# A decoder step on one core: first right-hand block in its own tile, x by quarters, norm sums by token, w_out low parts from DRAM, a feed forward that begins with one half of the tokens

## Chip, core and metric

The kernel runs on one core of a Trainium2 chip. The metric is the device time of one execution in microseconds; the number quoted is the median of three. A profile of one execution shows what the engines did: TensorE (PE, matmuls; its weight loads are PEld), VectorE (DVE), ScalarE (ACT), GpSimd (POOL), and SyncE (SP), which issues the DMAs.

## What is computed

One layer of a decoder for 1024 prompt tokens and 8 single sample tokens, 1032 columns in all. The first half of the program (input projection, attention, pooling) is not touched. The part that matters here:

```
m = sigmoid(gate_a) * a + sigmoid(gate_b) * bb      # a: attention output through w_attn_o
x = x + gt1 * (m @ w_out)
h2 = _rmsnorm(x, g_norm2) * (1 + sc2) + sh2
gg, up = jnp.split(h2 @ w_gu, 2, axis=-1)
x = x + gt2 * ((jax.nn.silu(gg) * up) @ w_down)
```

The model width is 1024 (8 blocks of 128), the feed-forward width 2816 (22 blocks). All arithmetic is to f32 accuracy.

## The kernel before

**Products.** A matrix product of f32 accuracy is made of three matmuls: each operand is split into a high part (ACT copies it to the narrower type, line 100) and a low part (the difference, line 109, on DVE or POOL); high x high, high x low and low x high are summed in PSUM. In the feed forward, each product of 2x2 blocks is in addition computed with seven block products in place of eight, from sums and differences of blocks.

**Order.** The program is written as one list; a scheduler gives each engine its own queue, by priorities and estimates. Each queue runs strictly in its order: an instruction whose wait is open holds up all that stand behind it. The same holds for SP, which issues all the DMAs named here.

**Tokens by halves and quarters.** The columns are two halves i = 0 and 1 of 516, each two quarters of 258 (`T2` = 516, `HC` = 258). Matmuls here have 258 columns.

**`back`, first part.** `heads` loads an attention output of head pair k and half i from DRAM (`ot` from `o_d`) and splits it to `os`. For half 1 the three finished pairs are multiplied by `wo` while attention still runs, and ACT stores the result in `six` (lines 1070 to 1078). After attention, all of half 0 is multiplied (`pj`, 24 matmuls for each of 8 output blocks j), DVE applies gate a, POOL adds the gate b term (line 1052), and the result is split into `mh` and `ml`. For half 1, `rest` does the fourth pair while w_out runs on half 0.

**`back`, w_out and norm.** For half 0 and then half 1: eight blocks of `wout` are loaded and split (the low part by DVE or POOL, `WOE`; in both passes), multiplied by `mh` and `ml` (48 matmuls a block), DVE adds gate and residual (`x1a`, `x1b`), the result goes to `x1_d` in DRAM, ACT squares it (line 1199), the square is split into `sqh` and `sql`, and `stat` sums it over the partitions by matmuls with a matrix of ones (line 1173; the last block in f32, line 1170). `norm` takes the root (ACT) and the reciprocal (DVE, line 1104, 128 x 516), multiplies the eight blocks by it, applies scale and shift, and makes the seven combinations `cmb` of the feed forward's right-hand side. `norm(0)` runs beside the w_out pass of half 1; `norm(1)` runs when that pass is done, beside the feed forward's first group.

**`feed_forward`, groups.** 22 groups f, each 7 products x 2 halves x 12 = 168 matmuls, in PSUM tiles `fb`, `fa`, `fd`. Evictions: ACT copies `p1`, `u2`, `u4`; DVE line 1288 adds `p1` into the first entry of `stg`; lines 1301 and 1308 add to `u4`, `u2`; POOL multiplies. PE starts the sixth product on `fb` when `u4` has been copied out. `p1`, `u2`, `u4` have two buffers each, one for each half. In an even f the first right-hand block is written to entry 0 of `stg`; in the odd f the rest; at the end of the odd f DVE forms the sums (lines 1312 to 1315), and one DMA a half (line 1316, 903 KB) writes all seven entries to `cmb_d` in DRAM. `stg` has one buffer a half:

```
st = [ev.tile([P, 7, HC], F32, name="stg", tag=f"stg{i}", bufs=1) for i in range(2)]
```

Group 0 is followed by eight small `gate_late` products (`ada`); groups 1 to 12 also load w_down blocks and store their sums (`ws_d`).

**`feed_forward`, down.** Seven products o, each 264 matmuls (`fc`). Each needs eleven blocks `cml`, one for each pair of groups, loaded from `cmb_d`, split to `bh` and `bl`. `xacc` (eight loads of 516 KB, lines 1335 to 1339) brings x back from DRAM for the final sum.

## Time and profile before

| | |
|---|---|
| median of three runs | 1819.63 us (1814.4 to 1821.92) |
| the profiled execution | 1823.61 us |
| its span in the trace | 1821.8 us |
| mean granted PE clock over the span | 0.971 of full |

The trace is read as follows. Times in it are microseconds from the start of the span. Attention ends near 900, the w_out passes run from about 928 to 1058, the feed forward's group 0 from 1061, groups 1 to 21 from 1107.7 to 1578.4, the down product from there to the end at 1821.8. In a window row the count behind an engine's busy time includes instructions that overlap an edge. PEclk is the share of the full 2.4 GHz that PE was granted.

### The profile page before, as it was taken

The page shows a single profiled execution, that of the slowest core. Times are in us where ns is not written, and L with a number is a line of the kernel's source. Part 1 is how long each engine was busy: PE and PEld are TensorE (multiplying, and loading weights), DVE is VectorE, ACT ScalarE, POOL GpSimd, SP SyncE. Part 2 cuts the span into 40 slices and gives each one's busy share as a digit, 9 for nine tenths or more (in the row PEclk, how much of TensorE's full clock was granted, in tenths as well). Part 3 has the DMA queues.
Part 4 walks back from the last instruction along what each step waited for, and adds up shares of the span by engine and source line. Part 5 has one row for each costly group of instructions (what it writes and reads, how often), then busy time and mean ns, then how long its engine had stood idle before and what let it go on. Part 6 is the DMA issues. An engine that isn't in the chain of part 4 may idle for free. (4 is left out here: it accounts for less than half of the span.)

```text
span 1821.8 us, 34407 instructions
## 1 busy us (share of the span) xinstructions
PE 1688.4 (93%) x12936; PEld 1586.4 (87%) x12936; DVE 1014.5 (56%) x1947; ACT 773.5 (42%) x1875; POOL 527.5 (29%) x501
## 2 busy tenths in 40 slices
PE   6799999999999999998899879899989999969999
PEld 5799899789697899997799769899989999869999
DVE  6656756557241456557677865555454444545553
ACT  5433555445341445557634653333333333433431
POOL 2424201011011323222153526766564333100000
PEclk9899999999999999999999989899999999989999
DMA  9113634535635434214465325555552333665662
GB/s 372 63 58 104 218 99 136 172 111 155 194 114 182 155 122 128 95 65 131 129 213 164 112 86 188 178 169 177 171 169 87 93 112 111 203 235 171 222 195 75
DMA packets 172697, 270.12 MB, mean 148 GB/s; under 512 B 19017, under 2 KB 123106, under 8 KB 171506
## 3 DMA queue, kind: packets, MB, share of 16 engines
q1 hardware_dynamic: 172530, 267.92, 46.7%
q8 instruction: 102, 1.67, 0.4%
q14 instruction: 65, 0.53, 0.1%
HBM read 202.82 MB, written 65.04 MB: 147 GB/s over the span
## 5 line engine op out<-in xcount | busy, mean ns | idle before, releaser
L1255 PE MATMUL fb<-cmb,wst 128*128 128x258 f32 x704 | 207.9, 295 | 35.8 <-ACT u L1300 26.3
L1256 PE MATMUL fb<-cmb,wst 128*128 128x258 f32 x704 | 205.6, 292 | 0.7 <-DVE cmb L109 0.7
L1257 PE MATMUL fb<-cmb,wst 128*128 128x258 f32 x704 | 204.6, 291 | 0.0
L1255 PE MATMUL fc<-bh,wdn 128*128 128x258 f32 x616 | 174.4, 285 | 17.1 <-ACT bh L100 17.1
L1255 PEld LDWEIGHTS fb<-cmb,wst 128*128 128x128 f32 x704 | 139.7, 198 | 40.6 <-ACT u L1300 29.2
L1256 PE MATMUL fc<-bl,wdn 128*128 128x258 f32 x616 | 174.6, 284 | 0.0
L1257 PE MATMUL fc<-bh,wdn 128*128 128x258 f32 x616 | 173.1, 283 | 0.0
L70 PE MATMUL pj<-hh,wt_hi 128*128 128x344 f32 x480 | 159.4, 332 | 0.5 <-ACT u L546 0.5
L71 PE MATMUL pj<-hl,wt_hi 128*128 128x344 f32 x480 | 157.0, 327 | 0.0
L72 PE MATMUL pj<-hh,wt_lo 128*128 128x344 f32 x480 | 156.9, 327 | 0.0
L70 PE MATMUL kn<-wuh,lh 128*128 128x256 f32 (+1 forms) x512 | 150.4, 294 | 2.4 <-ACT nr L906 1.5
L71 PE MATMUL kn<-wul,lh 128*128 128x256 f32 (+1 forms) x512 | 145.3, 284 | 0.0
L72 PE MATMUL kn<-wuh,ll 128*128 128x256 f32 (+1 forms) x512 | 144.9, 284 | 0.0
L905 ACT ACTIVATE dsq<-kn 128x256 f32<-128x256 f32 x256 | 95.0, 380 | 111.2 <-PE kn L72 103.5
L1256 PEld LDWEIGHTS fb<-cmb,wst 128*128 128x128 f32 x704 | 139.7, 198 | 1.4 <-DVE cmb L109 1.4
L1257 PEld LDWEIGHTS fb<-cmb,wst 128*128 128x128 f32 x704 | 139.1, 198 | 0.0
L109 DVE TENSOR_TENSOR wst<-scm,wst 128x512 fp32r<-128x512 f32 x88 | 81.0, 922 | 93.2 <-ACT wst L100 91.7
L1255 PEld LDWEIGHTS fc<-bh,wdn 128*128 128x128 f32 x616 | 116.8, 190 | 17.5 <-ACT bh L100 17.3
L1256 PEld LDWEIGHTS fc<-bl,wdn 128*128 128x128 f32 x616 | 117.4, 191 | 0.0
L1257 PEld LDWEIGHTS fc<-bh,wdn 128*128 128x128 f32 x616 | 116.3, 190 | 0.3 <-DVE wdn L109 0.3
L907 DVE TENSOR_REDUCE ssq<-dsq 128x8 f32<-128x512 f32 x128 | 86.7, 679 | 53.0 <-ACT dsq L905 52.6
L70 PEld LDWEIGHTS kn<-wuh,lh 128*128 128x128 f32 x512 | 96.6, 189 | 13.5 <-issue 5.2
(397 smaller groups left out, 5106.5 us busy)
## 6 DMA issues: line engine op xcount, KB each, us to landing
fraw<-wgu_t SPq DMA_DIRECT2D x44, 512.0 KB, 4.1
cmb_d<-stg SPq DMA_DIRECT2D x22, 903.0 KB, 5.9
cml<-cmb_d SPq DMA_DIRECT2D x77, 258.0 KB, 3.5
pg<-cpack SPq DMA_DIRECT2D x128, 144.0 KB, 2.6
ln<-cnat SPq DMA_DIRECT2D x128, 128.5 KB, 2.3
wraw<-wada_t SPq DMA_DIRECT2D x24, 512.0 KB, 4.5
wraw<-win_t SPq DMA_DIRECT2D x20, 512.0 KB, 4.0
nat_d<-nat SPq DMA_DIRECT2D x8, 1024.0 KB, 4.5
```

The lines of the kernel that those rows point to most:

```text
L70: nc.tensor.matmul(out, sh, mh, start=first, stop=False)
L71: nc.tensor.matmul(out, sh, ml, start=False, stop=False)
L72: nc.tensor.matmul(out, sl, mh, start=False, stop=last)
L109: e.tensor_tensor(dl, src, dh.bitcast(F32), op=ALU.subtract)
L905: nc.scalar.activation(sq[:, half].rearrange("p h d -> p (h d)"), kn[:, o:o + 256], AF.Square)
L907: nc.vector.tensor_reduce(ssq[:, j, t], sq.rearrange("p a h d -> p (a h) d"), axis=AX.X, op=ALU.add)
L1255: nc.tensor.matmul(acc, sh, mh, start=first and not more, stop=False, **kw)
L1256: nc.tensor.matmul(acc, sh, ml, start=False, stop=False, **kw)
L1257: nc.tensor.matmul(acc, sl, mh, start=False, stop=last, **kw)
```

## The change

The change has five parts.

1. *w_o and gates.* `os` of half 0 for the first three pairs goes to tiles of pool M instead of tiles that weights use later, and so it may be split during attention. `six` now receives gate a from DVE (`gated`) and gate b from POOL during attention, so `rest` is one DVE operation and one POOL addition. The `pm` PSUM tile is two banks in one buffer.
2. *w_out low parts.* In the pass of half 0 each low part is also written to `wlo_d` in DRAM; in the pass of half 1 it is loaded from there and copied by ACT. The `wout` tiles rotate over three pairs instead of two.
3. *Norm sums.* POOL adds the squares of blocks 0 to 6 into `tot`; `rms` then sums `tot` and the last square over partitions with twelve matmuls of one column, the token on the output's partition; root and reciprocal are 86 x 6; six matmuls with the identity spread the result over the partitions, and DVE multiplies from PSUM.
4. *Feed forward.* The body of a group is a function of the halves; group 0 runs with half 0 alone, then the `ada` products, then half 1. The first right-hand block has its own tile `b11`, written by ACT and stored by its own DMA in the even f; `stg` has six entries and is opened in the odd f. Line 1292 of the new kernel adds in place in `p1`.
5. *x by quarters.* `xacc` is four loads of 1 MB, the first of them into a tile `xq` that is free when the w_down sums are done; each is issued ahead of the product that needs it.

```diff
+        wlo_d = self.dram.tile([8, P, 8, P], F32, name="wlo_d")
...
-            pm = r.enter_context(tc.tile_pool(name="pm", bufs=2, space=PSUM))
+            pm = r.enter_context(tc.tile_pool(name="pm", bufs=1, space=PSUM))
...
-            six = [m(f"c1_{8 + j}", "six") for j in range(8)]
+            six = [m(f"c1_{8 + j}", "part") for j in range(8)]
...
+                ot = m(f"c1_{22 + i}" if k == 3 else ("c1_22", "c1_23", "c0_23")[k], "ot")
                 nc.sync.dma_start(two(ot), seg(self.o_d[k], i))
-                if i == 0 and k < 3:
-                    z = self.W.tile([P, 2, T2], F32R, name="os", tag=f"w{k}")
-                    os[i][k] = [z[:, 0], z[:, 1]]
-                else:
-                    os[i][k] = [m(f"c0_{24 + 2 * i + n}" if k == 3 else f"c1_{2 * k + n}", "os", F32R) for n in range(2)]
+                os[i][k] = [m(f"c0_{24 + 2 * i + n}" if k == 3 else f"c1_{(0 if i else 16) + 2 * k + n}", "os", F32R)
+                            for n in range(2)]
                 self.split(*os[i][k], ot, "a")
...
+            def gated(t, g, acc):
+                nc.vector.scalar_tensor_tensor(two(t), two(g), 1.0, acc, op0=ALU.add, op1=ALU.mult)
...
             def rest(j):
                 t = self.sp.tile([P, T2], F32, name="mt", tag=f"s{j % 4}")
+                g = gate(self.sga_d, 1, j, xo.tile([P, T2], F32, name="sa2", tag=f"x{j}"))
+                acc = pm.tile([P, 2, 512], F32, name="pm", tag="pm")[:, :, :HC]
                 for h in range(2):
                     cs = slice(h * HC, (h + 1) * HC)
-                    acc = pm.tile([P, 512], F32, name="pm", tag="pm")[:, :HC]
-                    _mm3(nc, acc, *last(j), os[1][3][0][:, cs], os[1][3][1][:, cs], True, True)
-                    nc.vector.tensor_tensor(t[:, cs], acc, six[j][:, cs], op=ALU.add)
-                nc.vector.scalar_tensor_tensor(t, sa[1][j], 1.0, t, op0=ALU.add, op1=ALU.mult)
-                mix(1, j, t)
+                    _mm3(nc, acc[:, h], *last(j), os[1][3][0][:, cs], os[1][3][1][:, cs], True, True)
+                gated(t, g, acc)
+                mix(1, j, t, six[j])
...
+                g, b = (gate(d, 1, j, m(f"c0_{8 * n + j}", "early")) for n, d in enumerate((self.sga_d, self.gB_d)))
+                acc = pm.tile([P, 2, 512], F32, name="pm", tag="pm")[:, :, :HC]
                 for h in range(2):
                     cs = slice(h * HC, (h + 1) * HC)
-                    acc = pm.tile([P, 512], F32, name="pm", tag="pm")[:, :HC]
                     for k in range(3):
-                        _mm3(nc, acc, w[0][:, k], w[1][:, k], os[1][k][0][:, cs], os[1][k][1][:, cs], k == 0, k == 2)
-                    nc.scalar.activation(six[j][:, cs], acc, AF.Copy)
+                        _mm3(nc, acc[:, h], w[0][:, k], w[1][:, k], os[1][k][0][:, cs], os[1][k][1][:, cs], k == 0,
+                             k == 2)
+                gated(six[j], g, acc)
+                nc.gpsimd.tensor_tensor(six[j], six[j], b, op=ALU.add)
...
+            def rms(sums):
+                z = ps.tile([P, 2, 512], F32, name="st2", tag="mm")
+                n = HC // 3
+                for c in range(6):
+                    for q, t in enumerate(sums):
+                        nc.tensor.matmul(z[:n, 0, 300 + c:301 + c], t[:, c * n:c * n + n], self.ones[:, 0:1],
+                                         start=(q == 0), stop=(q == len(sums) - 1))
+                rs = xw.tile([P, 6], F32, name="rs2", bufs=1)
+                nc.scalar.activation(rs[:n], z[:n, 0, 300:306], AF.Sqrt, scale=1.0 / DM, bias=self.eps[:n])
+                nc.vector.reciprocal(rs[:n], rs[:n])
+                for c in range(6):
+                    nc.tensor.matmul(z[:, c // 3, c % 3 * n:c % 3 * n + n], rs[:n, c:c + 1].to_broadcast([n, P]),
+                                     self.ident[:n, :n], start=True, stop=True)
+                return z[:, :, :HC]
+            def norm(i, x1, sums, cm, tiles):
+                rb = rms(sums)
                 yield
                 def act(j):
                     x = x1[j]
-                    nc.vector.tensor_tensor(x, x, rs, op=ALU.mult)
+                    nc.vector.tensor_tensor(two(x), two(x), rb, op=ALU.mult)
...
+                tot = xw.tile([P, T2], F32, name="tot")
...
-                    wh, wlo = (self.W.tile([P, 8, P], F32R, name="wout", tag=f"w{3 + 2 * (j % 2) + n}") for n in range(2))
-                    self.split(wh, wlo, raw, "a", WOE[j])
+                    wh, wlo = (self.W.tile([P, 8, P], F32R, name="wout", tag=f"w{1 + 2 * (j % 3) + n}") for n in range(2))
                     if i == 0:
-                        gates_in(1, j)
+                        self.split(wh, wlo, raw, "a", WOE[j])
+                        nc.sync.dma_start(wlo_d[j], wlo.bitcast(F32))
+                    else:
+                        self.hi("a", wh, raw)
+                        raw = fw.tile([P, 8, P], F32, name="fraw")
+                        nc.sync.dma_start(raw, wlo_d[j])
+                        self.hi("a", wlo, raw)
...
-                    sq = xw.tile([P, T2], F32, name="sq2", bufs=1)
+                    sq = xw.tile([P, T2], F32, name="sq2") if j else tot
                     nc.scalar.activation(sq, x, AF.Square)
-                    if j == 7:
-                        sqs.append(sq)
-                    else:
-                        sqs.append([xw.tile([P, T2], F32R, name=z, tag=z) for z in ("sqh", "sql")])
-                        self.split(*sqs[j], sq, "a")
-                    if j:
-                        stat(j - 1)
+                    if 0 < j < 7:
+                        nc.gpsimd.tensor_tensor(tot, tot, sq, op=ALU.add)
                     for _ in range(3):
                         next(todo, None)
-                stat(7)
                 for _ in todo:
                     pass
                 self.comb.append(self.combos(i))
-                todo = norm(i, x1, st, self.comb[i], temps)
+                todo = norm(i, x1, (tot, sq), self.comb[i], temps)
...
-                if f % 2 == 0:
-                    st = [ev.tile([P, 7, HC], F32, name="stg", tag=f"stg{i}", bufs=1) for i in range(2)]
-                    b12 = [ev.tile([P, HC], F32, name="b12", tag=f"b12{i}", bufs=1) for i in range(2)]
-                    n1, n2 = [z[:, 0] for z in st], b12
-                else:
-                    n1, n2 = [z[:, 1] for z in st], [z[:, 5] for z in st]
-                b, p1, u2, u4, d = ([None, None] for _ in range(5))
-                for i in range(2):
+                for i in halves:
+                    if f % 2:
+                        st[i] = ev.tile([P, 6, HC], F32, name="stg", tag=f"stg{i}", bufs=1)
+                        n1[i], n2[i] = st[i][:, 0], st[i][:, 4]
+                    else:
+                        n1[i] = e1[i] = ev.tile([P, HC], F32, name="b11", tag=f"b11{i}", bufs=1)
+                        n2[i] = e2[i] = ev.tile([P, HC], F32, name="b12", tag=f"b12{i}", bufs=1)
+                for i in halves:
                     b[i] = bank("fb")[:, :HC]
                     run(b[i], 0, i)
                     p1[i] = t("p1")
...
-                    nc.vector.tensor_tensor(n1[i], a, p1[i], op=ALU.add)
-                for i in range(2):
+                    nc.vector.tensor_tensor(p1[i], a, p1[i], op=ALU.add)
...
-                    nc.scalar.activation(n1[i], n1[i], AF.Silu)
-                for i in range(2):
+                    nc.scalar.activation(n1[i], p1[i], AF.Silu)
...
-                    if f % 2:
+                    if f % 2 == 0:
+                        nc.sync.dma_start(self.cmb_d[0, f // 2, :, i], n1[i])
+                    else:
                         z, tt = st[i], nc.vector.tensor_tensor
-                        tt(z[:, 4], b12[i], z[:, 0], op=ALU.subtract)
-                        tt(z[:, 3], z[:, 5], b12[i], op=ALU.subtract)
-                        tt(z[:, 2], z[:, 5], z[:, 4], op=ALU.subtract)
-                        tt(z[:, 6], z[:, 1], z[:, 2], op=ALU.subtract)
-                        nc.sync.dma_start(self.cmb_d[:, f // 2, :, i].rearrange("o p n -> p o n"), z)
+                        tt(z[:, 3], e2[i], e1[i], op=ALU.subtract)
+                        tt(z[:, 2], z[:, 4], e2[i], op=ALU.subtract)
+                        tt(z[:, 1], z[:, 4], z[:, 3], op=ALU.subtract)
+                        tt(z[:, 5], z[:, 0], z[:, 1], op=ALU.subtract)
+                        nc.sync.dma_start(self.cmb_d[1:7, f // 2, :, i].rearrange("o p n -> p o n"), z)
+            for f in range(NF):
+                if f:
+                    w = weights(f)
+                    group(f, w, (0, 1))
+                else:
+                    group(f, w, (0,))
                 if f == 0:
                     for k in range(40, 48):
                         self.gate_late(k, ev, bank)
+                    group(f, w, (1,))
...
+        def xload(dm, h):
+            z = (xp if xs else xq).tile([P, 4, T2], F32, name="xacc", tag=f"xa{dm}_{h}" if xs else "xq")
+            nc.sync.dma_start(z, self.x1_d[dm:dm + 4][:, :, h * T2:(h + 1) * T2].rearrange("a p n -> p a n"))
+            for j in range(4):
+                xs[dm + j, h] = z[:, j]
...
+            if (dm, h) not in xs:
+                xload(dm, h)
```

**Order on DVE, turn of a pair of groups.** Before: the rows from the end of an odd f (`stg_15562`) to the even f that follows (`stg_16072`); `wst` are weight splits of the next group.

```order
L1315 TENSOR_TENSOR stg_15562<-stg_15562 128x258
L1315 TENSOR_TENSOR stg_15563<-stg_15563 128x258
L109 TENSOR_TENSOR wst_16303<-fraw_16291,wst_16303 128x512
L109 TENSOR_TENSOR wst_16306<-fraw_16291,wst_16306 128x512
L1288 TENSOR_TENSOR stg_16072<-fa_16106,p1_16089 128x258
L109 TENSOR_TENSOR wst_16309<-scm_16296,wst_16309 128x512
L1288 TENSOR_TENSOR stg_16073<-fa_16120,p1_16104 128x258
L109 TENSOR_TENSOR wst_16312<-scm_16297,wst_16312 128x512
L1301 TENSOR_TENSOR u4_16202<-fd_16162,u4_16202 128x258
L1301 TENSOR_TENSOR u4_16217<-fd_16176,u4_16217 128x258
```

Now, at a turn between an odd and an even f:

```order
L1321 TENSOR_TENSOR stg_15777<-stg_15777 128x258
L1321 TENSOR_TENSOR stg_15778<-stg_15778 128x258
L109 TENSOR_TENSOR wst_16270<-fraw_16258,wst_16270 128x512
L1292 TENSOR_TENSOR p1_16054<-fa_16071,p1_16054 128x258
L1292 TENSOR_TENSOR p1_16069<-fa_16085,p1_16069 128x258
L109 TENSOR_TENSOR wst_16273<-fraw_16258,wst_16273 128x512
L109 TENSOR_TENSOR wst_16276<-scm_16263,wst_16276 128x512
L109 TENSOR_TENSOR wst_16279<-scm_16264,wst_16279 128x512
L1305 TENSOR_TENSOR u4_16167<-fd_16127,u4_16167 128x258
L1305 TENSOR_TENSOR u4_16182<-fd_16141,u4_16182 128x258
```

Before, the sum behind the `fa` product wrote `stg_16072`, which lies in the buffer of `stg_15562`, the tile that the DMA behind the line 1315 rows reads. Now it writes `p1`, and the even f names no `stg` until line 1318, six rows further on.

**Order on ACT, entry of the feed forward.** `cmb` are the high parts of `norm(1)`, `p` is the first eviction of the group, `ada_e` belongs to the `ada` products. Before:

```order
L100 ACTIVATE cmb<-x1b 128x258 x4
L100 ACTIVATE cmb<-tcm 128x516 x5
L1284 ACTIVATE p_13434<-fb 128x258
L1284 ACTIVATE p_13449<-fb 128x258
L182 ACTIVATE ada_e<-ada_ps 128x128 x2
L1296 ACT_TABLE_LOAD
L1296 ACTIVATE stg<-stg 128x258 x2
L1292 ACTIVATE u_13491<-fb 128x258
L1292 ACTIVATE u_13505<-fb 128x258
L1300 ACTIVATE u_13547<-fb 128x258
```

Now:

```order
L100 ACTIVATE cmb<-x1b 128x258 x4
L100 ACTIVATE cmb<-tcm 128x516 x5
L1288 ACTIVATE p_13377<-fb 128x258
L182 ACTIVATE ada_e<-ada_ps 128x128 x2
L1300 ACT_TABLE_LOAD
L1300 ACTIVATE b_13362<-p_13377 128x258
L1296 ACTIVATE u_13405<-fb 128x258
L182 ACTIVATE ada_e<-ada_ps 128x128 x2
L1304 ACTIVATE u_13433<-fb 128x258
```

The evictions of half 0 stand alone, and the `cmb` copies stand ahead of them as they did. On PE, the rows ahead of the group's first matmul (`fb`) are now these:

```order
L1105 MATMUL st_13247<-ones,sq_13184 86x1
L1105 MATMUL st_13247<-ones,tot 86x1
L1105 MATMUL st_13247<-ones,sq_13184 86x1
L1105 MATMUL st_13247<-ones,tot 86x1
L1105 MATMUL st_13247<-ones,sq_13184 86x1
L1111 MATMUL st_13247<-c_ident,rs_13260 128x86 x6
L1256 MATMUL fb<-cmb,wst 128x258
L1257 MATMUL fb<-cmb,wst 128x258
L1258 MATMUL fb<-cmb,wst 128x258
```

The matmul rows `st<-c_ident` fill the PSUM tile that DVE's multiplications read.

**Order on SP, end of the feed forward.** Before:

```order
L1369 DMA cml<-cmb_d 128x516 x2
L1316 DMA cmb_d<-stg 128x7x258 x2
L1378 DMA fraw<-wdn_t 128x640
L1338 DMA xacc<-x_d 128x1032 x8
L1369 DMA cml<-cmb_d 128x516
L1378 DMA fraw<-ws_d 128x768
L1369 DMA cml<-cmb_d 128x516
L1378 DMA fraw<-ws_d 128x640
```

Now:

```order
L1386 DMA cml<-cmb_d 128x516 x2
L1322 DMA cmb_d<-stg 128x6x258 x2
L1386 DMA cml<-cmb_d 128x516
L1397 DMA fraw<-wdn_t 128x640
L1397 DMA fraw<-ws_d 128x768
L1386 DMA cml<-cmb_d 128x516
L1356 DMA xacc<-x_d 128x4x516 x3
L1397 DMA fraw<-ws_d 128x640
```

The `cml` row that stood behind the eight `xacc` loads now stands ahead of three larger ones, and there are two weight loads between the `stg` DMAs and it; the `cml` blocks of the first product are all ahead of the `stg` DMAs.

## Rows read from the trace of the kernel before

**Rows 1.** the page's part 1: busy time, share of the span, instructions

```profile
PE 1688.4 (93%) x12936; PEld 1586.4 (87%) x12936; DVE 1014.5 (56%) x1947; ACT 773.5 (42%) x1875; POOL 527.5 (29%) x501
```

**Rows 2.** windows: length, busy (count) of PE, PEld, DVE, ACT, POOL; PEclk, DMA, GB/s

```profile
900.00:920.00 20.00, 13.25 (x69) 12.05 (x69) 8.37 (x13) 6.76 (x11) 3.68 (x2) 0.66 0.72 245
920.00:1000.00 80.00, 78.27 (x641) 77.29 (x639) 61.51 (x85) 32.07 (x45) 35.01 (x21) 1.00 0.59 174
1000.00:1020.00 20.00, 11.56 (x80) 11.29 (x80) 18.88 (x35) 11.26 (x20) 6.83 (x4) 0.83 0.35 105
1020.00:1060.00 40.00, 36.34 (x295) 35.52 (x293) 29.72 (x44) 21.41 (x36) 18.46 (x13) 1.00 0.41 130
1060.00:1107.70 47.70, 34.41 (x315) 30.29 (x313) 27.44 (x54) 22.28 (x50) 15.38 (x12) 0.89 0.24 78
1107.70:1179.60 71.90, 65.75 (x504) 65.09 (x505) 46.19 (x51) 25.64 (x57) 55.97 (x42) 0.91 0.63 203
1179.60:1386.40 206.80, 189.53 (x1514) 188.07 (x1513) 109.44 (x156) 67.24 (x153) 125.98 (x108) 0.96 0.53 165
1386.40:1578.40 192.00, 186.39 (x1526) 185.13 (x1525) 96.17 (x163) 74.63 (x163) 65.49 (x65) 0.99 0.38 109
1578.40:1613.00 34.60, 17.51 (x129) 16.85 (x128) 11.72 (x23) 5.61 (x10) 3.15 (x4) 0.75 0.77 262
```

**Rows 3.** windows: one feed-forward group of 168 matmuls without a wait

```profile
1159.40:1179.60 20.20, 20.20 (x171) 20.20 (x170) 10.95 (x16) 7.68 (x17) 13.71 (x11) 1.00 0.47 157
```

**Rows 4.** PE's waits from 900 to 1110: line, releaser, total, times, longest

```profile
PE st L1173 <- ACT sqh L100: 7.5, 2, 6.2
PE pj L70 <- ACT os L100: 5.3, 1, 5.3
```

**Rows 5.** groups by line, POOL from 900 to 1060, then DVE

```profile
L109 POOL TENSOR_TENSOR wout<-fraw,wout 128x1024 fp32r<-128x1024 f32 x10 | 26.2, 2616 | 56.0 <-ACT wout L100 31.9 <-DMA fraw<-wout_t 19.9 <-DMA xr<-xT 4.2
L1052 POOL TENSOR_TENSOR mt<-gb,mt 128x516 f32<-128x516 f32 x16 | 24.1, 1510 | 26.1 <-DVE mt L1064 12.0 <-DVE mt L1097 8.5 <-issue 2.9
...
L109 DVE TENSOR_TENSOR sql<-sq,sqh 128x516 fp32r<-128x516 f32 x14 | 13.7, 978 | 6.0 <-ACT sqh L100 6.0
```

**Rows 6.** single lines: count, ns min/median/max, first and last start

```profile
L1104 DVE RECIPROCAL rstd<-rstd x2: 3378/3378/3378, 998.3 to 1061.0; 128x516 f32<-128x516 f32 x2
...
L286 PE MATMUL n<-ones,rstd x18: 163/352/373, 17.7 to 21.2; 128*128 128x1 f32 x16, 128*8 128x1 f32 x2
...
L299 PE MATMUL rb<-c_ident,rs x18: 175/356/582, 23.5 to 26.8; 128*128 128x128 f32 x16, 128*128 128x8 f32 x2
...
L1314 DVE TENSOR_TENSOR stg<-stg x22: 416/870/1516, 1134.4 to 1582.5; 128x258 f32<-128x258 f32 x22
```

**Rows 7.** windows of DVE alone, the last part of attention

```profile
852.00:900.00 48.00, 32.81 (x91) 0.96 0.39 111
```

**Rows 8.** timeline of ACT, feed forward entry: start, length, [idle <-releaser]

```profile
1085.66 0.66 ACT L1284 ACTIVATE p<-fb 128x258 f32<-128x258 f32 x2 [3.07 <-DVE cmb L109]
```

**Rows 9.** waits of PE, then of DVE, from 1107 to 1578

```profile
PE fb L1255 <- ACT u L1300: 26.3, 12, 5.9
...
DVE stg L1288 <- DMA cmb_d<-stg: 66.3, 20, 6.9
```

**Rows 10.** timeline of DVE, then of PE, in one even group

```profile
1331.05 0.43 DVE L1288 TENSOR_TENSOR stg<-fa,p 128x258 f32<-128x258 f32 x1 [4.50 <-DMA cmb_d<-stg]
...
1336.69 0.58 PE L1255 MATMUL fb<-cmb,wst 128*128 128x258 f32 x1 [5.91 <-ACT u L1300]
```

**Rows 11.** chain of waits at the feed forward's end: start, length, what

```profile
1586.16 8.37 DMA cmb_d<-stg
...
1598.44 9.59 DMA cml<-cmb_d
...
1608.73 1.23 PE fc L1255 x4
```

More of the change, by code (lines that the diff above doesn't have):

```diff
@@ L1096, in back @@
                 t = self.sp.tile([P, T2], F32, name="mt", tag=f"s{j % 4}")
[L1097 to L1104 removed]
+                gated(t, sa[j], acc)
+                mix(0, j, t, gb[j])
+            def rms(sums):
[14 more added lines that the diff above has]
+                rb = rms(sums)
                 yield
@@ L1156, in temps @@
                     return [s, [m(f"c1_{24 + k}", "tcm") for k in range(4)]]
-                return [s, [xw.tile([P, T2], F32, name="tcm", tag=t) for t in ("sqh", "sqh", "sql", "sql")]]
+                return [s, [xw.tile([P, T2], F32, name="tcm", tag="tcm", bufs=4) for k in range(4)]]
             self.comb, todo = [], iter(())
             for i in range(2):
-                st = ps.tile([P, 2, 512], F32, name="st2", tag="mm")[:, :, :HC]
                 x1 = [xo.tile([P, T2], F32, name="x1b", tag=f"x{j}") if i else m(f"c1_{16 + j}", "x1a")
                       for j in range(8)]
-                sqs = []
-                def stat(j):
-                    for h in range(2):
-                        cs = slice(h * HC, (h + 1) * HC)
-                        if j == 7:
-                            nc.tensor.matmul(st[:, h], self.ones, sqs[j][:, cs], start=False, stop=True)
-                        else:
-                            for n in range(2):
-                                nc.tensor.matmul(st[:, h], onesr, sqs[j][n][:, cs], start=(j == 0 and n == 0), stop=False)
+                tot = xw.tile([P, T2], F32, name="tot")
                 for j in range(8):
@@ L1261, in feed_forward, with group @@
             units = [(j, p0, n) for j in range(4) for p0, n in ((0, 4), (4, 4), (8, 3))]
-            st, b12 = [None, None], [None, None]
-            for f in range(NF):
-                if f:
-                    w = weights(f)
+            st, e1, e2 = [None, None], [None, None], [None, None]
+            def group(f, w, halves):
+                b, p1, n1, n2, u2, u4, d = ([None, None] for _ in range(7))
                 def run(acc, o, i, more=False):
@@ L1301, in feed_forward @@
                     nc.vector.tensor_tensor(u4[i], d[i], u4[i], op=ALU.add)
-                for i in range(2):
+                for i in halves:
                     run(b[i], 5, i, True)
@@ L1305, in feed_forward @@
                     nc.gpsimd.tensor_tensor(n2[i], n2[i], u4[i], op=ALU.mult)
-                for i in range(2):
+                for i in halves:
                     run(d[i], 6, i, True)
```

53 lines of the change are left out of this document (19 added, 34 removed).

## Prediction

> **What bounds the kernel now.** I read the page's busy times first, then windows cut at the stages, then the waits of the stages that lose time, and last the chain of waits at the end of the feed forward. PE is busy for 93% of the span [rows 1], so the other engines count only where PE waits for them. One feed-forward group without a wait takes 20.2 us for 168 matmuls [rows 3], 0.12 us each. With that price every window of [rows 2] gives a loss, its length less its matmul count times 0.12:
>
> - end of attention, 900 to 920: 20 - 69 x 0.12 = 11.7 us, 5.3 of it the wait for `os` [rows 4], much of the rest the clock (0.66 in that window).
> - w_out, 920 to 1060: 80 - 76.9 = 3.1, then 20 - 9.6 = 10.4, then 40 - 35.4 = 4.6, in all 18 us. DVE is busy for 18.9 of the 20 us from 1000 to 1020; the longest wait is 6.2 us of `stat` for the split squares [rows 4].
> - entry, 1060 to 1107.7: PE is idle for 13.3 of 47.7 us and the clock is 0.89.
> - groups 1 to 21, 1107.7 to 1578.4: 470.7 - 21 x 20.2 = 46.5 us. PE waits 26.3 us for the copy `u4` in twelve places; DVE waits 66.3 us at line 1288 for the DMA that reads `stg` [rows 9]. One place shows the link: the DVE row ends 4.5 us of waiting, and PE then ends 5.9 us [rows 10]. The addition to `u4` stands behind line 1288 in DVE's queue, and a `u4` buffer comes free only by it. The other 20 us lie mostly in a lower clock behind these gaps (0.91 and 0.96 in the windows).
> - turn to the down product, 1578.4 to 1613: 34.6 - 129 x 0.12 = 19.1 us. The chain is DMA of `stg` 8.4 us, SP issuing eight `xacc` loads, then one `cml` load of 9.6 us beside them, then PE [rows 11].
>
> **Part by part.**
>
> *w_o and gates.* `os` of three pairs is ready early, so nine matmuls (3 pairs x 3) may run before PE meets the fourth pair, which still waits for attention's last output. That saves 9 x 0.12 = 1.1 us and some of the splits behind it: -2. Against it, attention's last part gets eight DVE operations and eight POOL additions (1.5 us each [rows 5]), and sixteen more gate loads. DVE has 15 of 48 us free there [rows 7], which covers eight operations of 0.8 us. A DVE row shows what a POOL operation beside it can do: the same 128x258 subtraction takes 0.42 to 1.52 us [rows 6]. So the price lies between nothing and 8 x 1.1 = 8.8 us of DVE time, inside the free time, of which I let at most 5 reach PE. I take +1: sum -1, bounds -2 and +3.
>
> The Trainium skill ("SBUF — State Buffer", section "SBUF: two separate sides") says that DVE with two SBUF inputs and GpSimd share one pair of ports, and that the loser blocks for the whole instruction. By that rule the eight additions would hold DVE up each time, and this part would come to +3 instead of -1; the stretch of 0.42 to 1.52 us in the trace [rows 6] agrees with it.
>
> *w_out and norm sums.* DVE loses fourteen `sql` of 0.98 us [rows 5] and two reciprocals of 3.4 us [rows 6], in the second pass about 7 + 3.4 + three low splits, 14 of some 40 busy us between 996 and 1042. ACT loses the `sqh` and gains eight copies of `wout` in the second pass; it is busy for 11.3 of 20 us there, so it covers them. POOL gains twelve additions of 1.5 us (18 us) and loses five splits of 2.6 us [rows 5], 13 us, all of the second pass. PE loses 56 ones-matmuls at 0.12 (6.7 us) and eight in f32 (at most 3), and gains 24 of one column at 3.5 / 18 = 0.2 us and 12 of 86 at 3.3 / 18 = 0.18 us [rows 6], 7.0 us: -1.5. The stalls of 18 us hang on DVE's queue, which keeps its `norm(0)` bursts; I leave 5 us of them, for the new matmuls wait in PE's queue for POOL's last addition and for the root. So -13 - 1.5, taken as -14; bounds -18 (nothing left) and -4 (the stall only moves to the new sums, one wait of 6 us in each pass as before).
>
> *Entry.* The first `fb` matmul now waits until DVE has done all eight multiplications, since they read the PSUM tile that it takes; it starts some 8 us later than before. That by itself costs nothing, because the first eviction waits for the last low split of `norm(1)` before (3.1 us, until 1085.7 [rows 8]) and, by the order on ACT, after. Until then half 0 offers only 36 matmuls (three products; the fourth needs the eviction) and 40 small ones, where before both halves offered 72 and 16: 36 x 0.12 = 4.3 us move behind 1085.7, less 24 small ones. Then half 0 and half 1 each run alone, and the copy between two products on one bank (0.3 us of ACT for each [rows 8], plus two hand-overs) is no longer covered by the other half: about four places of 0.7 us, 2.8, partly filled by the `ada` rows. The reciprocal's 3.4 us do not return, as the two small matmul rounds take about as long. Net +2.5, bounds -3 (the smaller reciprocal counts in full) and +7 (4.3 + 2.8).
>
> *Groups.* Line 1292 writes `p1`, so no DVE row waits for the `stg` DMA before the first subtraction of the odd group's sums, a group after its issue (20 us against 8.4 [rows 11]). The 66 us of DVE waits go, and with them PE's 26.3 and the clock behind them. What is late next: the `b11` DMAs wait on SP for POOL at the end of each even group, and weight loads stand behind them; they are split a group later, which covers 4 to 9 us of transfer. POOL is busy for 126 of 207 us in groups 4 to 12 [rows 2]. I leave 6.5 of the 46.5 us: -40, bounds -44 and -28 (as much as the clock and short waits lose from 1386 on, 10.2 us in 192, and double that in the first part).
>
> *Turn to the down product.* The last block of the first product comes from an even group, one group earlier; PE has 264 x 0.12 = 31.7 us of matmuls before it needs the second product. The chain that it hides is 7 us of DVE (`stg` is done at 1586.2, PE at 1578.4), 8.4, at most 9.6, and 1 of ACT, 26 us. So the 17 us wait and its clock go: -19, bounds -19 and -14 (x loads of the same bytes hold up the weights by 5 us).
>
> *Sum:* -1 - 14 + 2.5 - 40 - 19 = -71.5. The profiled execution took 1823.6 us, 4.0 above the median: 1752.1 there, **1748** on the median's scale.
>
> **Rivals.**
>
> *The entry gains.* Half 0 hides `norm(1)`, and PE's idle 13.3 us shrink by 10: 1748 - 12.5 = 1735.5. The order on ACT speaks against it: the first eviction stands behind every `cmb` copy. 8%.
>
> *The groups wait for the next thing.* POOL's product, SP's `b11` DMA or the splits take half of the place of the `stg` wait: groups -28, w_out -4, the rest as above: -49.5, 1770. For it speaks that POOL is busy for 56 of 72 us in the window behind the entry; against it, that one group with POOL at 13.7 of 20.2 us ran without a wait [rows 2, 3]. 20%.
>
> *It does less than it says.* The subtraction that opens `stg` in an even group still finds the old DMA open (it took 4.5 us too long even with the start of the group as the limit [rows 10]) and the groups give only -10: -41.5, 1778. A limit some 15 us later speaks against it. 7%.
>
> *Slower than before.* SP's queue: each `b11` DMA waits for POOL, and the weight loads behind it come too late for every group. Each group would then lose what the worst place loses, 5.9 us [rows 10]: 22 x 5.9 = 130 instead of 46.5, so +83 - 31.5 = +52, 1871. It decides from (46.5 + 31.5) / 22 = 3.5 us a group. Against it stands the lead of a group. 3%.
>
> **How the numbers follow.** The forecast has 60% and its own range is 1736 to 1764. The rivals have 8, 20, 7 and 3%; 2% are for no change by offsets that I don't see. The range 1734 to 1778 takes in the second rival and reaches the first and third. About 0.5%, 9 us, is what a measurement of this kernel can tell from no change: faster 0.95, within it 0.02, slower 0.03.
>
> **What would show it.** In the profile of the changed kernel: groups 1 to 21 in 424 to 432 us, and no DVE wait on `cmb_d` at line 1292; no idle of PE beyond 2 us at the first `fc` of the second product; fewer than 7 us lost from 920 to 1060; the first eviction still behind the last `cmb` split, and the entry no shorter than 46 us. I would be wrong if PE waits for `wst` in even groups, if POOL's `tot` holds the norm sums, or if the entry shrinks.

## The result

| | before | changed |
|---|---|---|
| median | 1820.78 us (1814.4 to 1822.31, 4 runs) | 1778.07 us (1775.73 to 1780.24, 4 runs) |
| profiled execution / span | 1823.61 / 1821.8 | 1777.11 / 1775.3 |

The ratio of the means is 0.9772 (0.9744 to 0.9799); the median is 42.7 us lower, where I had forecast 72, and a hair outside the range at its upper end. I cut both traces at five points that each kernel has (the start of each): the last `av` matmul of attention, the last w_out matmul, the first `fb`, the first `fa` of group 2 and of group 21.

| us | attention ends | to last w_out | to first `fb` | to group 2 | groups 2 to 21 | to the end |
|---|---|---|---|---|---|---|
| before | 900.9 | 156.4 | 3.8 | 71.5 | 425.5 | 263.7 |
| changed | 905.9 | 136.5 | 20.2 | 60.6 | 407.1 | 245.0 |
| difference | +5.0 | -19.9 | +16.4 | -10.9 | -18.4 | -18.7 |

The six differences add up to the 46.5 us between the spans. Nineteen groups without a wait would take 383 us, so the groups still lose 24 (42.5 before).

The windows of the changed kernel, as in [rows 2]: length, busy time (count) of PE, PEld, DVE, ACT, POOL, then PEclk, DMA share, GB/s:

```profile
905.90:1042.40 136.50, 127.76 (x1045) 126.32 (x1045) 86.64 (x126) 64.58 (x97) 64.49 (x44) 0.99 0.69 224
1042.40:1062.60 20.20, 6.87 (x38) 6.32 (x37) 13.95 (x22) 7.40 (x14) 2.74 (x2) 0.57 0.20 74
1120.30:1348.90 228.60, 213.62 (x1707) 211.94 (x1706) 121.94 (x173) 74.26 (x171) 145.63 (x125) 0.96 0.56 176
1348.90:1530.30 181.40, 181.40 (x1514) 181.40 (x1514) 95.11 (x159) 70.21 (x156) 73.43 (x71) 1.00 0.38 108
1541.80:1575.00 33.20, 31.80 (x259) 30.96 (x257) 22.32 (x41) 13.77 (x24) 4.16 (x4) 1.00 0.85 263
```

The whole loss of the groups lies up to group 12 (228.6 - 1707 x 0.12 = 24 us), where w_down blocks are loaded and summed; from 1349 on there is none. The turn to the down product [rows 11] has lost its 17 us. Waits of DVE, then of PE, from 1123 to 1530, to be set beside [rows 9]:

```profile
DVE stg L1318 <- POOL b L1313: 28.3, 6, 7.4
DVE stg L1319 <- POOL stg L1309: 16.7, 6, 5.6
...
PE fb L1256 <- ACT u L1296: 15.0, 8, 3.4
```

The wait for the `stg` DMA is gone, and DVE now waits for POOL. One place (timelines of POOL, DVE, ACT, PE, in that order) shows how this reaches PE:

```profile
1181.57 1.29 POOL L1232 TENSOR_TENSOR dsum<-fraw 128x512 f32<-128x512 f32 x1 [5.78 <-DMA fraw<-wdn_t]
...
1187.45 1.29 POOL L1234 TENSOR_TENSOR scm<-fraw 128x512 f32<-128x512 f32 x1 [1.52 <-DMA fraw<-wgu_t]
...
1193.81 1.44 POOL L1313 TENSOR_TENSOR b<-b,u 128x258 f32<-128x258 f32 x2
...
1194.58 0.95 DVE L1318 TENSOR_TENSOR stg<-b,b 128x258 f32<-128x258 f32 x1 [7.41 <-POOL b L1313]
...
1197.20 0.74 DVE L1292 TENSOR_TENSOR p<-fa,p 128x258 f32<-128x258 f32 x2
...
1197.64 0.42 ACT L1300 ACTIVATE stg<-p 128x258 f32<-128x258 f32 x1 [9.43 <-DVE p L1292]
...
1199.21 0.58 PE L1256 MATMUL fb<-cmb,wst 128*128 128x258 f32 x1 [3.36 <-ACT u L1296]
```

POOL's product `b11` stands behind sums that wait for weight loads. The subtraction of line 1318 needs it, and stands on DVE ahead of the `p1` additions of the odd group; the Silu and, behind it on ACT, the `u2` copy wait for those, and PE for the copy.

At the end of the second w_out pass (timelines of PE, then of DVE):

```profile
1046.95 0.45 PE L1105 MATMUL st<-ones,tot 128*86 128x1 f32 x2 [4.38 <-POOL tot L1208]
1050.70 0.45 PE L1105 MATMUL st<-ones,sq 128*86 128x1 f32 x2 [3.30 <-ACT sq L1206]
...
1062.61 0.55 PE L1256 MATMUL fb<-cmb,wst 128*128 128x258 f32 x1 [5.09 <-DVE x1b L1122]
...
1042.39 1.49 DVE L109 TENSOR_TENSOR cmb<-x1a,cmb 128x258 fp32r<-128x258 f32 x1
...
1047.97 1.28 DVE L109 TENSOR_TENSOR wst<-scm,wst 128x512 fp32r<-128x512 f32 x2
1049.18 0.74 DVE L1199 SCALAR_TENSOR_TENSOR x1b<-pj,mod,xr 128x516 f32<-128x516 f32 x1
```

PE finishes the pass 20 us sooner, counted from attention's end, but DVE is still busy with `norm(0)` and weight splits: the last eviction comes 6.8 us after the last matmul, and then the sums, the root and eight multiplications stand between it and the first `fb`.

### The profile page after: what moved, and what is told of

Same layout as the page of the kernel before. It is cut to its first block, busy times and chain, and to the rows that moved or that the text cites. A ratio compares the mean times of both kernels' runs of the same rounds, so it can differ in the third digit from the quotient of the medians.

```text
span 1775.3 us, 34467 instructions
## 1 busy us (share of the span) xinstructions
PE 1676.5 (94%) x12944; PEld 1577.8 (89%) x12944; DVE 994.8 (56%) x1922; ACT 764.0 (43%) x1852; POOL 533.5 (30%) x516
## 5 line engine op out<-in xcount | busy, mean ns | idle before, releaser
L1256 PE MATMUL fb<-cmb,wst 128*128 128x258 f32 x704 | 205.1, 291 | 25.8 <-ACT u L1296 15.0
L1257 PE MATMUL fb<-cmb,wst 128*128 128x258 f32 x704 | 203.6, 289 | 0.0
L1258 PE MATMUL fb<-cmb,wst 128*128 128x258 f32 x704 | 203.1, 289 | 0.0
L1256 PEld LDWEIGHTS fb<-cmb,wst 128*128 128x128 f32 x704 | 137.9, 196 | 29.0 <-ACT u L1296 16.7
L1257 PEld LDWEIGHTS fb<-cmb,wst 128*128 128x128 f32 x704 | 138.1, 196 | 0.0
L1258 PEld LDWEIGHTS fb<-cmb,wst 128*128 128x128 f32 x704 | 137.8, 196 | 0.0
```

The costliest lines, as they stand in the source:

```text
L1256: nc.tensor.matmul(acc, sh, mh, start=first and not more, stop=False, **kw)
L1257: nc.tensor.matmul(acc, sh, ml, start=False, stop=False, **kw)
L1258: nc.tensor.matmul(acc, sl, mh, start=False, stop=last, **kw)
```

## Experiments

The kernels ran beside the kernel before on chips where that one takes 1830 to 1833 us; so ratios to it are compared, and stretches of the traces. Of each edit only the lines that matter are shown.

**The changed kernel again (e5_same).**

> The changed kernel itself once more, beside the next three on one chip. Expected: a ratio of 0.974 to 0.980 to the kernel before, groups 2 to 21 with 22 to 33 us of loss; if the loss of the groups differs by more than 8 us from the 24 us of the first profile, it is not a fixed sum but varies with the transfers.

Ratio 0.9750 (0.9731 to 0.9770); groups 2 to 21 took 411.8 us, 28.8 lost. In the seven profiles that have the groups as changed (this one, the first, and experiments 6, 7 and 8) the loss is 24 to 33 us, so a difference of a few us between two profiles says nothing.

The expectations of experiments 1, 2 and 9 count the groups by wider cuts (430 us in the changed kernel, where the table above has 407.1): 23 us come off theirs. The first `fb` to group 2 is 57.7 by theirs and 60.6 by the table's.

**1. First subtraction made last (e1_dep).**

```diff
-tt(z[:, 3], e2[i], e1[i], op=ALU.subtract)
 tt(z[:, 2], z[:, 4], e2[i], op=ALU.subtract)
-tt(z[:, 1], z[:, 4], z[:, 3], op=ALU.subtract)
+tt(z[:, 1], z[:, 2], e1[i], op=ALU.add)
+tt(z[:, 3], z[:, 4], z[:, 1], op=ALU.subtract)
```

> The changed kernel, with the three sums of the odd group written so that each needs the odd group's own product: the first block b12 - b11 is made last, from z4 - z1. So the DVE row that needs POOL's product b11 can no longer stand ahead of the p1 additions (line 1292) of the odd group. Theory 1 (the order on DVE: line 1318 waits for POOL's b11 product, 28 us in groups 2 to 12, and line 1292, the Silu and the u2 copy stand behind it): PE's 15 us of waiting for the u2 copy fall below 4, groups 2 to 21 go from 430 to 408-414 us, time 1756 to 1764. Rival (weights come late from DRAM, POOL is late for that reason, and PE would wait for the next thing anyway): groups 2 to 21 stay above 424 us, time 1772 to 1780.

Ratio 0.9679 (0.9655 to 0.9703), groups 397.8 us, 14.8 lost: between the theories. PE's wait for the `u2` copy fell only from 15.0 to 11.6 us. The wait at `b11` was gone, but the next row that needs POOL, the odd group's own product, now held DVE instead (waits of PE, then of DVE):

```profile
PE fb L1256 <- ACT u L1296: 11.6, 5, 4.6
...
DVE stg L1318 <- POOL stg L1309: 26.2, 6, 6.7
```

**2. Gate products on DVE (e2_mulv).**

```diff
-nc.gpsimd.tensor_tensor(n2[i], n2[i], u4[i], op=ALU.mult)
+nc.vector.tensor_tensor(n2[i], n2[i], u4[i], op=ALU.mult)
...
-nc.gpsimd.tensor_tensor(n1[i], n1[i], u2[i], op=ALU.mult)
+nc.vector.tensor_tensor(n1[i], n1[i], u2[i], op=ALU.mult)
```

> The changed kernel, with the two gate products of each group on DVE instead of POOL (88 rows of 0.4 us more on DVE, about 1.8 us a group of 20). Line 1318 then waits for nothing on another engine. Theory 1 (DVE waits for a POOL that is behind on weight sums): the DVE wait on POOL is gone, groups 2 to 21 take 408 to 416 us, time 1757 to 1766. Rival (late weights hold PE in any case): groups 2 to 21 above 424 us, time 1772 to 1780, with the waits on ACT wst or DMA fraw in place of those on the u2 copy.

Ratio 0.9580 (0.9560 to 0.9601), better than expected. The window over groups 2 to 21, and a wait of POOL in it:

```profile
1125.70:1508.90 383.20, 383.20 (x3194) 383.14 (x3193) 262.04 (x406) 145.65 (x326) 156.04 (x115) 1.00 0.54 156
...
POOL dsum L1232 <- DMA fraw<-wdn_t: 29.8, 5, 6.7
```

PE is busy all the time: nothing is lost, though DVE does 46 us more. POOL still waits for its loads as it did (27.4 us for these in the changed kernel, 29.8 here), and that holds up nothing once DVE doesn't wait for POOL.

**3. Even groups' products alone on DVE (e13_even).**

```diff
-nc.gpsimd.tensor_tensor(n2[i], n2[i], u4[i], op=ALU.mult)
+(nc.gpsimd if f % 2 else nc.vector).tensor_tensor(n2[i], n2[i], u4[i], op=ALU.mult)
```

(and the same for `n1`)

> The changed kernel, with the gate products of the even groups alone on DVE (44 of 88); those of the odd groups stay on POOL. Theory 1a (the cost is the DVE wait for POOL's product b11 ahead of the p1 additions): 28 us of DVE waiting at line 1318 go, the 16.7 us at line 1319 stay, which held PE little: groups 2 to 21 lose 0 to 8 us (24 in the changed kernel), ratio to the kernel before 0.959 to 0.965. Rival 1b (POOL has too much to do and to wait for as a whole): the wait moves to the odd groups' products and 12 to 20 us stay lost, ratio 0.967 to 0.973.

Ratio 0.9654 (0.9637 to 0.9670), 391.9 us, 8.9 lost, both a hair above what theory 1a gave; the wait at line 1319 stayed:

```profile
DVE stg L1319 <- POOL stg L1309: 20.6, 6, 8.1
```

Theory 1a holds for the larger part (24 to 33 lost before, 9 now); what is left is the same wait once more, at the odd group's product.

**4. w_down sums on DVE (e14_dsv).**

```diff
-tt = self.nc.gpsimd.tensor_tensor
+tt = (eng or self.nc.gpsimd).tensor_tensor
...
-                              raws[1][:, 4:4 + n])
+                              raws[1][:, 4:4 + n], nc.vector)
```

> The changed kernel, with the sums of the w_down blocks on DVE instead of POOL (48 rows of about 0.6 us), all gate products on POOL as in the changed kernel. Theory 1c (POOL is late because w_down sums stand ahead of the products in its queue and wait for their loads): the products come in time, the wait at line 1318 is below 5 us, groups 2 to 21 lose 0 to 8 us, ratio 0.958 to 0.966. Rival (DVE now waits itself for the same loads, ahead of the p1 additions): 15 to 35 us stay lost, with DVE waits on DMA fraw, ratio 0.968 to 0.982.

Ratio 0.9739 (0.9723 to 0.9755), 409.9 us, 27 lost. Theory 1c falls in the form in which it was put: without the w_down sums POOL waited for the loads of the next group's weights, and the wait for its product was as long (waits of POOL, then of DVE):

```profile
POOL scm L1234 <- DMA fraw<-wgu_t: 112.6, 9, 16.6
...
DVE stg L1318 <- POOL b L1313: 26.9, 6, 5.9
DVE dsum L1232 <- DMA fraw<-wdn_t: 24.0, 9, 5.2
```

The rival came true as well: DVE now waits 24 us for the same loads itself. So this run does not show what less work on POOL alone would give; it shows that the w_down sums are not the only thing that makes the product late.

**5. The tile b11 alone, on the kernel before (e10_b11).**

```diff
-    n1, n2 = [z[:, 0] for z in st], b12
+    n1, n2 = b11, b12
...
-nc.vector.tensor_tensor(n1[i], a, p1[i], op=ALU.add)
+nc.vector.tensor_tensor(p1[i], a, p1[i], op=ALU.add)
...
+nc.sync.dma_start(self.cmb_d[0, f // 2, :, i], n1[i])
```

> The kernel before with one edit: the first right-hand block of an even group in its own tile b11, with its own store, and stg of six entries opened in the odd group. Theory 1: the 66 us of DVE waits for the stg DMA go, but the first subtraction now waits for POOL's product ahead of the p1 additions, so groups 2 to 21 lose 22 to 33 us instead of 46 (before, with group 1); and the first down product no longer waits at its eleventh block, but the second still does behind eight x loads: 17 us of idle become 0 to 8. Ratio to the kernel before 0.980 to 0.987. Rival (the tile alone gives what I had forecast for the groups, and the wait for POOL comes from other parts of the change): groups 2 to 21 lose less than 10 us, ratio 0.966 to 0.975.

Ratio 0.9800 (0.9780 to 0.9820). Groups 2 to 21 took 410.6 us, with the same wait, and the stretch to the end fell from 263.7 to 243.8 us. A window from the first `fc` on, and the wait of DVE:

```profile
1555.90:1590.00 34.10, 33.65 (x278) 33.24 (x277) 20.93 (x38) 12.17 (x21) 3.95 (x4) 1.00 0.89 279
...
DVE stg L1315 <- POOL b L1310: 32.8, 8, 7.9
```

So the tile alone gives the whole gain at the turn, with the eight x loads as they were; x by quarters adds nothing that shows. It also gives 2.0 of the 2.5% that the changed kernel gains here, and it makes the wait for POOL by itself.

**6. Half entry undone (e3_both).**

```diff
-                    group(f, w, (0,))
+                    group(f, w, (0, 1))
...
-                    group(f, w, (1,))
```

> The changed kernel, with group 0 run on both halves at once and the ada products behind it, as before; everything else as changed. Theory 2 (entering with one half costs, since half 0 alone offers 36 matmuls until the first eviction and then runs without the other half as cover): the stretch from the first fb matmul to the start of group 2 shrinks from 57.7 to 52-56 us, time 1772 to 1777. Rival (the single half gains, since norm(1) is hidden behind it): the stretch grows to 62-68 us, time 1782 to 1788.

Ratio 0.9741 (0.9720 to 0.9761). From the first `fb` to group 2 it took 59.4 us, against 60.1 to 60.8 in the kernels that differ from the changed one in other places (those with the old norm sums and those of experiment 9 left out): neither theory; by this one profile the half entry costs about 1 us there.

**7. Early gates undone (e4_gates).**

```diff
-                g, b = (gate(d, 1, j, m(f"c0_{8 * n + j}", "early")) for n, d in enumerate((self.sga_d, self.gB_d)))
...
-                gated(six[j], g, acc)
-                nc.gpsimd.tensor_tensor(six[j], six[j], b, op=ALU.add)
+                    nc.scalar.activation(six[j][:, cs], acc[:, h], AF.Copy)
```

> The changed kernel, with the gates of half 1 applied as before (six is a plain copy by ACT during attention; gate loads, addition and product come with the w_out pass). Theory 3 (sixteen early gate loads, 4 MB within 20 us, and the DVE and POOL work of the gates delay attention's last part): the last av matmul goes from 905.9 back to 900-902 us, with the DMA share from 820 to 840 at 0.65-0.75 instead of 0.95; the time falls by 2 to 5 us, unless the w_out pass gives it back (six DVE and ACT rows more). Rival (attention's end moved because os of half 0 is now split there): the last av matmul stays at 904-907 us and the time at 1776 to 1781.

Ratio 0.9721 (0.9697 to 0.9744). Attention ended at 900.0; in all the kernels with the gates as before it ended at 899.9 to 903.9, in all those with early gates at 905.9 to 911.0. So the early gates cost attention time, 5.0 us in the profiles of the result. Theory 3 gave two reasons, the loads and the gates' work on DVE and POOL, and this edit takes back both. The windows from 820 to 840, of the kernel before, the changed one and this run:

```profile
820.00:840.00 20.00, 15.53 (x92) 13.17 (x92) 15.71 (x52) 14.51 (x40) 5.91 (x7) 0.91 0.67 222
...
820.00:840.00 20.00, 15.15 (x74) 12.38 (x72) 13.75 (x41) 13.57 (x36) 4.11 (x5) 0.74 0.95 316
...
820.00:840.00 20.00, 13.85 (x65) 11.40 (x66) 14.26 (x41) 14.02 (x39) 3.77 (x5) 0.75 0.62 205
```

The DMA share fell back from 0.95 to 0.62, yet PE did no more matmuls in this window, at the same clock: it does not show that the crowd of loads held PE up. The two kernels part later, from 860 to 900 (changed, then this run); there, from 861 to 893, DVE and POOL of the changed kernel do the gates:

```profile
860.00:900.00 40.00, 37.86 (x286) 35.31 (x286) 34.68 (x89) 25.58 (x70) 19.77 (x18) 1.00 0.37 109
...
860.00:900.00 40.00, 40.00 (x310) 38.34 (x309) 30.06 (x84) 30.17 (x87) 8.74 (x10) 0.99 0.44 131
```

This speaks for the work rather than the loads, but no run takes back one without the other. What attention gains is kept up to the feed forward: the first copy `p` comes 171.4 us after attention's end (172.5 in the changed kernel), and group 2 begins 7 us sooner. In this execution the groups then lost 29.6 us, and the end took 2 us more; whether the total gains can't be told from the ratios.

**8. Norm sums undone (e6_norm), low parts undone (e7_wlo), all three undone (e9_three).**

```diff
-                    if 0 < j < 7:
-                        nc.gpsimd.tensor_tensor(tot, tot, sq, op=ALU.add)
+                        self.split(*sqs[j], sq, "a")
+                    if j:
+                        stat(j - 1)
```
```diff
-                        nc.sync.dma_start(raw, wlo_d[j])
-                        self.hi("a", wlo, raw)
+                        self.split(wh, wlo, raw, "a", WOE[j])
```

> The changed kernel, with the norm sums as before: squares split into high and low parts on ACT and DVE, summed by PE with a matrix of ones, root and reciprocal 128 x 516. All else as changed. Theory 4 (these splits and the two reciprocals filled DVE in the second w_out pass, and the stalls of PE there came from them): PE loses 8 us or more again between the two w_out passes' ends, the last w_out matmul comes 8 to 14 us later against attention's end (136.5 us in the changed kernel), the first fb matmul 3 to 10 us later, ratio to the changed kernel 1.002 to 1.006. Rival (the copies of the low parts and the earlier gates removed the stalls): the last w_out matmul moves by less than 4 us and the first fb matmul comes earlier, since the sums of the last block no longer wait for POOL and two rounds of small matmuls; ratio 0.995 to 1.000.

> The changed kernel, with the low parts of w_out split again in the second pass (three on DVE at 1.5 us, five on POOL at 2.6 us) instead of loaded from DRAM and copied by ACT. Theory 5 (POOL and DVE are behind at the end of the second pass, and each us there delays the first fb matmul): the first fb matmul comes 4 to 12 us later, ratio to the changed kernel 1.002 to 1.007. Rival (the copies only move work to ACT, which the sums wait for as well): within 3 us either way, ratio 0.998 to 1.002.

> The changed kernel with three parts taken back at once: the early gates, the copied low parts and the norm sums are as in the kernel before (os of half 0, three pairs of w_out tiles, the feed forward and x by quarters stay as changed). From attention's end to the first copy p the kernel before takes 184.8 us, the changed one 172.0, and each part alone taken back left 171 to 173. Theory 7 (the three relieve DVE between the end of the first w_out pass and norm(1), and two of them are enough): this stretch returns to 180 us or more, ratio to the changed kernel 1.001 to 1.005 (attention's end comes 6 to 10 us earlier). Rival (what is left, the tiles of os and the third pair of w_out tiles, made the gain): the stretch stays at 171 to 175 us, ratio 0.992 to 0.997.

| us | ratio | attention's end to last w_out | to first `fb` | to group 2 | attention's end to first copy `p` |
|---|---|---|---|---|---|
| changed again | 0.9750 | 136.0 | 20.1 | 60.3 | 171.9 |
| gates undone | 0.9721 | 141.5 | 14.2 | 60.5 | 171.4 |
| norm sums undone | 0.9745 | 141.4 | 6.7 | 71.3 | 172.7 |
| low parts undone | 0.9734 | 143.3 | 13.1 | 60.7 | 172.1 |
| all three undone | 0.9831 (0.9815 to 0.9848) | 163.4 | 3.7 | 71.3 | 191.8 |

Each part alone saves PE 5 to 7 us in the pass and gives them back before the first `fb`; the copy `p`, which needs `norm(1)` done, comes at the same time in all four. With all three undone it comes 20 us later. So theories 4 and 5 fall for a part taken alone, and theory 7 holds in that any two are enough; the total, 0.8% above the changed kernel's, lies above the 0.1 to 0.5% that it gave. Which chain then sets the 172 us was not shown, nor why all three undone come out 7 us above the 184.8 of the kernel before.

**9. Better versions (e8_mgw, e11_mg, e12_mgp).** All have the products on DVE and the gates as before; e8 writes the weights of group 0 behind `norm(1)`, e12 has their low parts made by POOL.

```diff
-            first = weights(0)
             for _ in todo:
                 pass
+            first = weights(0)
```
```diff
-            self.split(w[:, 0:n], w[:, 4:4 + n], src, "a")
+            self.split(w[:, 0:n], w[:, 4:4 + n], src, "a", leng)
```

> Three edits on the changed kernel: both gate products of a feed-forward group on DVE, the gates of half 1 as in the kernel before, and the weight sums and splits of group 0 written behind norm(1) instead of ahead of it. Theory 6 (the last two evictions x1b stand behind weight splits on DVE: 6.6 us from the last w_out matmul to the last eviction): the first fb matmul comes 11 to 14 us after the last w_out matmul instead of 20, attention's end 6 to 9 us earlier, groups 2 to 21 without loss (403 to 406 us); ratio to the kernel before 0.947 to 0.953. Rival (the splits are wanted by group 0 anyway and come late then): the gain up to the first fb matmul is lost before group 2, ratio 0.953 to 0.958.

> Two edits on the changed kernel: both gate products of a group on DVE, and the gates of half 1 as in the kernel before. If the gains add: attention's end 6 to 9 us earlier, groups 2 to 21 without loss, ratio to the kernel before 0.953 to 0.957 (the products on DVE alone gave 0.958). If the early gates were worth it for the w_out passes, the ratio stays at 0.957 to 0.961.

> As the run before, and the low parts of group 0's weights made by POOL instead of DVE (seven rows of 0.65 us on DVE go, the last two evictions x1b no longer stand behind them; POOL was idle for 15.7 us there). Theory 6 (DVE's queue at the end of the second w_out pass sets the first copy p): last w_out matmul to first copy p falls from 35 to 28-32 us, ratio to the run before 0.996 to 0.998. Rival (POOL now holds up the norm sums, or the weights come late as they did when they were written behind norm(1)): the stretch to group 2 is not shorter, ratio 0.999 to 1.004.

Ratios 0.9606 (0.9577 to 0.9635), 0.9581 (0.9565 to 0.9597) and 0.9582 (0.9566 to 0.9598). In e8 the first `fb` came 12.1 us after the last w_out matmul, but PE then waited for the weights:

```profile
PE fd L1256 <- ACT wst L100: 8.8, 1, 8.8
```

The rival's mechanism held, though the ratio is a little above what either theory gave. In e11 attention ended at 901.1, and group 2 began 6.8 us sooner than in e2 (1118.9 against 1125.7); the ratio of e2, 0.9580, is the same even so, and the intervals leave room for some 4 us either way, so whether the two gains add is not shown. e12 was no faster from attention's end to group 2 (221.8 us, 217.8 in e11). The products on DVE are the gain; with them alone (e2) the kernel is 1.7% faster than the changed one (0.9580 to 0.9750).

## Why the prediction missed

- **Groups: -40 forecast, -18.4 measured** (with group 1 counted to the entry). This is the step that failed, and it is nearly the whole miss. What the tile was to remove is gone: no DVE row waits for the `stg` DMA. The step that failed is "The 66 us of DVE waits go, and with them PE's 26.3 and the clock behind them", with 6.5 us left over. DVE waits for POOL in their place, 28.3 us at line 1318 and 16.7 at line 1319, PE still waits 15.0 us, and 24 us stay lost. I asked the first subtraction only about the DMA, and not about POOL's product, its other operand, though it stands in DVE's queue ahead of the odd group's `p1` additions. I had POOL late for SP's `b11` store alone. The second rival (20%, 1770) named half of the place and put the groups at -28. e10 shows that the tile alone makes the wait, e1, e2 and e13 show the link; why POOL is late (its sums wait for weight loads) is read from the traces alone. The bound of -28 does not come out of its own words either: 10.2 us and double that are 30.6 left of 46.5, a gain of 16. The third rival's time, 1778, is met by number only: its mechanism, the old wait for the DMA, is not there.
- **w_o and gates: -1 forecast, +5.0 measured at attention's end**, beyond the upper bound of +3. I let at most 5 us of the gates' work reach PE and did not price the sixteen loads. The Trainium skill's rule of the shared ports ("SBUF — State Buffer", "SBUF: two separate sides") gave +3; the trace shows such stretches again (a 128x258 split takes 1.49 us beside POOL's additions at 1042.4, where the shortest operation of that shape in [rows 6] took 0.42). How much of the 5 us here is this, and how much the loads, stays open (experiment 7).
- **w_out and norm sums: -14 forecast; -12.3 measured** from attention's end to the first copy `p` (184.8 to 172.5). The size was about right, the reasons were not, so this was luck: of three reliefs two suffice. The price of the new sums was misread as well: the rows of f32 matmuls in [rows 6] count two instructions for each matmul (nine in the code, x18 in the row), so that 3.5 / 18 halved it, to 0.2 from 0.39 us. The new ones cost neither. In the first pass, at a granted clock of 1.00 (2.4 GHz), a matmul of one column takes 0.15 us and one of 86 columns 1.47 / 6 = 0.25; in the second, at 0.50 (1.2 GHz), after PE has waited for POOL's last sum and for the last square, 0.29 and 2.86 / 6 = 0.48. The 36 of them cost about 9.7 us instead of 7.0.
- **Entry: +2.5 forecast.** From the copy `p` to group 2 it took 46.9 us before and 44.9 now, -2.0. That the first copy stays behind the last split of `norm(1)`, and that the late start of `fb` costs nothing by itself, held (after attention's end e6 starts `fb` 8 us sooner than e5 and reaches group 2 three us later). The price of the half entry was too high: undone, it gave about 1 us. Where the 2 us come from was not shown.
- **Turn: -19 forecast, -18.7 measured**, by the tile alone. The mechanism was right; the quarters of x had no part in it that shows.
- **Sum.** 5.0 - 12.3 - 2.0 - 18.4 - 18.7 = -46.4, for a forecast of -71.5: of the 25 us missing 21.6 are the groups' term, 6.0 the gates', 1.7 w_out's and 0.3 the turn's, less 4.5 at the entry.

## What to carry to other kernels

When a wait is taken from an in-order queue, go through every operand of each row that now stands at its place, and ask which engine makes it and what that engine has queued ahead. A row that is only filler, put where the scheduler believed its engine idle, must not wait for another engine in front of a row that the critical engine needs. And parts that work on the same stretch need not add: here, undone one at a time each looks worthless, and undone together 20 us return.

## What the runs showed that I had not expected

- 88 products of 128x258 put on DVE cost nothing that shows (DVE busy 262 of 383 us in groups 2 to 21) and left PE without one wait in 19 groups, while with the same products on POOL 24 to 33 us were lost. One such product took POOL 0.72 us; the longest wait of DVE for one was 7.4.
- Sixteen early loads of 258 KB took the DMA share from 0.67 to 0.95 over 20 us, and PE did fewer matmuls there at a lower clock. It looks like cause and effect, but without these loads, at a share of 0.62, the same window was no better (65 matmuls at a clock of 0.75).
- The f32 matmuls of one column follow each other at 0.15 us in the first pass and at 0.29 in the second, half as fast at half the granted clock (two windows, then timelines of PE from the first pass and from the second; each matmul shows as two instructions, so the six spreading ones stand as x12):

```profile
1007.00:1009.00 2.00, 2.00 (x20) 2.00 (x19) 0.49 (x2) 2.00 (x3) 0.00 (x0) 1.00 0.94 371
1050.70:1057.60 6.90, 6.25 (x34) 5.94 (x34) 0.65 (x3) 0.26 (x1) 0.00 (x0) 0.50 0.12 39
...
1002.71 0.29 PE L1105 MATMUL st<-ones,sq 128*86 128x1 f32 x2
1002.86 0.29 PE L1105 MATMUL st<-ones,tot 128*86 128x1 f32 x2
...
1007.47 1.47 PE L1111 MATMUL st<-c_ident,rs 86*128 86x86 f32 x12
...
1051.02 0.43 PE L1105 MATMUL st<-ones,tot 128*86 128x1 f32 x2
1051.31 0.43 PE L1105 MATMUL st<-ones,sq 128*86 128x1 f32 x2
...
1054.66 2.86 PE L1111 MATMUL st<-c_ident,rs 86*128 86x86 f32 x12 [0.57 <-DVE rs L1109]
```
